# One encoder block on one Trainium2 core: each head's keys written once from PSUM, and copied by DMA to the other half of the partitions

## The chip, the core and the metric

The kernel runs on one core of one Trainium2 chip. A core has TensorE (PE in the profile; weight loads have a row of their own, PEld), VectorE (DVE), ScalarE (ACT), GpSimd (POOL), and SyncE (SP), which here issues nearly all DMA transfers. PE writes to PSUM, ACT and DVE read it there, and both write to SBUF, the working memory of 128 partitions. The engines run side by side, each through its own instructions in a fixed order, and wait for each other by semaphores. The metric is device time in microseconds (us) for one execution of the whole block.

## The reference

One layer of a bidirectional encoder on 1024 positions of width 1024, batch 1, in float32. What matters here is the mixing half:

```python
h = rmsnorm(x, g_mix[i]) * (1 + scale1) + shift1
proj = h @ w_in[i]
qa, ka, va, qb, kb, vb, ga, gb = jnp.split(proj, split_at, axis=-1)
oa = mixture_of_dilations(heads(qa, 8), heads(ka, 8), heads(va, 8), rel_bias)
ob = neighbourhood_attention_2d(heads(qb, 8), heads(kb, 8), heads(vb, 8), na_rpb[i])
merged = sigmoid(ga) * (oa @ w_branch_dil[i]) + sigmoid(gb) * (ob @ w_branch_na[i])
x = x + gate1 * (merged @ w_out[i])
```

Eight heads of 64 channels attend in three dilated windows, merged by their denominators, and eight others in a two-dimensional window of 8 rows by 16 columns on a 16 x 64 grid. The scores are `q . k / 8 + bias`. A gated convolutional feed-forward half of width 2816 and a last RMSNorm follow; the change does not touch them.

## The kernel before

Products are kept near float32 accuracy with operands of 32-bit matmul type split in two: a high part `hi`, the value rounded to that type, and a low part `lo`, the rest. A projection is then three matmuls for each of eight blocks of the contraction (lines 77 to 79): `hi*hi`, `hi*lo` and `lo*hi`, 24 matmuls of 128 x 512 into one PSUM bank, named `pj`. Channels stand on the partitions and positions along the free axis, so one bank is a head pair (two heads of 64 channels) by half of the positions.

Scores use a trick of layout. A head has only 64 channels, so its 128-partition query tile `qs` holds the high part of q on one half of the partitions and the low part on the other. The key tile `ks` holds the high part of k, scaled by 1/8, on both halves, and `kl` the low part of k on both halves. Two matmuls then give all four products (lines 507 and 508, 537 and 538 in the dilated heads, 633 in the neighbourhood heads). For head `i` of a pair, the slice `a` is the half of the partitions on which its channels come out of the projection, and `b` the other half.

So the keys must stand twice in SBUF, and before the change all four are written straight from PSUM: `k_half` (line 390) takes one half of the positions and writes, for each of the two heads, `ks` twice on ACT (line 403) and `kl` twice on DVE (line 405). In the dilated heads a write is 64 x 512 in one run; in the neighbourhood heads the same number of elements is written in another order of grid columns and rows, with strides.

`qk_tiles` does this for one head pair: two halves of the queries, two halves of the keys. For the first pair it alternates query and key halves; for the others it does the queries, then the keys. There are eight pairs, 0 to 3 dilated and 4 to 7 neighbourhood. The loop of line 690 attends to pair n, then projects pair n + 1, then computes some gate tiles (`gate_tile`, line 676), two projections each, counted by `counts`: two tiles for each of the first four pairs, one for each of the next two, none for pair 6 and six for pair 7. The gates' results go to HBM as `gs`.

The PSUM pool `psg` has two banks for all these projections: a third one waits until the first has been read out. The pool `psl` has two banks for scores `S`; DVE adds the bias and takes minima (line 491 dilated, 637 neighbourhood), ACT takes the exponential (492, 639), PE transposes the result `P` into `T`, ACT and DVE split that into `th` and `tl` (496 and 497, 657 and 658), and PE multiplies with the values `vv` into `O`. `qkpool` has three buffers for each of `qs`, `ks` and `kl`, while one pair uses two.

Nobody wrote the order of the engines' instructions here by hand. The first stage (line 260) is in written order; from line 347 on a scheduler works out when it expects each instruction to be ready and merges the attention of pair n with the projections of pair n + 1 and the gates, for each engine, SP included. The order it finds is fixed when the program is built. A change of a few instructions can therefore move many others.

Beside the keys' reads of PSUM, SP's queue near the first pair matters: `vb_chunks` (line 446) copies the neighbourhood heads' values in 32 transfers from one HBM scratch tensor into four others, named `vb`, in the order that the later heads read.

Of the kernel before, what the change touches and what calls it, by code (L numbers as in the profile page):

```python
# [11 lines left out]
AF = mybir.ActivationFunctionType  # L12
OP = mybir.AluOpType
# [15 lines left out]
def hybrid_encoder(tc, xT, c, w_ada, small, w_in, w_v, p1_bias, p23_bias, na_bias, ln2_mult, ident, w_br, w_out,  # L29
                   w_up, w_down, out):  # L30
    nc = tc.nc
    act, dve, pool, pe, sp = nc.scalar, nc.vector, nc.gpsimd, nc.tensor, nc.sync
# [5 lines left out]
    def f(ap):  # L38
        return ap.bitcast(FT)
# [29 lines left out]
    def weights(src, lo_eng):  # L69
        return w_split(w_load(src), lo_eng)  # L70

    def product(psum, w, moving, k0=0, n=KT, ks=None):

        whi, wlo = w
        for k in ks or range(n):
            mhi, mlo = moving(k)
            pe.matmul(psum, whi[:, k0 + k], mhi, start=k == 0, stop=False)  # L77
            pe.matmul(psum, whi[:, k0 + k], mlo, start=False, stop=False)  # L78
            pe.matmul(psum, wlo[:, k0 + k], mhi, start=False, stop=k == n - 1)  # L79
# [89 lines left out]
    def x_load(hf):  # L169
        x = []  # L170
        for kp in range(4):
            t = x_tile() if hf == 0 else wpool.tile([128, S], FT, name=("whi", "wlo")[kp % 2])
            sp.dma_start(t.rearrange("p (a b) -> p a b", a=2), xT[hf, kp])
            x += [t[:, 512 * i:512 * i + 512] for i in range(2)]
        return x
# [84 lines left out]
    with tc.manual_schedule(engines={e.engine for e in (sp, act, dve, pool, pe)}):  # L260
        x = [x_load(0)]
# [49 lines left out]
        for n in range(24):  # L311
# [16 lines left out]
            i = n // 2 - 2  # L328
# [4 lines left out]
            if n % 2 and n >= 9:  # L333
                i = (n - 9) // 2
# [12 lines left out]
    def qk_tiles(br, pr, ws=None):  # L347
        qt, kt = ((0, 4), (12, 16))[br]
        qs = [qkpool.tile([128, S], FR, name="qs") for _ in range(2)]
        ks = [qkpool.tile([128, S], FR, name="ks") for _ in range(2)]  # L350
        kl = [qkpool.tile([128, S], FR, name="kl") for _ in range(2)]
        qb = []

        def q_half(hf, w, p=None):
            cols = halves[hf]
            if p is None:
                p = ps_g.tile([128, 512], FT, name="pj")
                if br == 0:
                    product(p, w, lambda k: h[hf, k])
                else:  # L360
                    q_windows(p, w, hf)
            for i in range(2):
                a, b = slice(64 * i, 64 * i + 64), slice(64 - 64 * i, 128 - 64 * i)
                d, pp = qs[i][:, cols], p
                if br:
                    d = qs[i].rearrange("p (v r t) -> p v r t", v=64, r=4)[:, :, 2 * hf:2 * hf + 2]
                    pp = p.rearrange("p (r v t) -> p v r t", r=2, v=64)
                act.activation(d[a], pp[a], AF.Copy)
                dve.tensor_tensor(d[b], pp[a], f(d[a]), OP.subtract)  # L369

        def q_windows(p, w, hf):

            whi, wlo = w
            for k in range(KT):
                mhi, mlo = (t.rearrange("p (r w c t) -> p r c w t", r=2, w=16, c=4) for t in h[hf, k])
                for x, (ww, m) in enumerate(((whi, mhi), (whi, mlo), (wlo, mhi))):
                    for r in range(2):
                        pe.matmul(p[:, 256 * r:256 * r + 256], ww[:, k], m[:, r], start=k + x + r == 0,  # L378
                                  stop=k == KT - 1 and x == 2, skip_group_check=True)

        def q_blocks():
            for i in range(2):
                q = qkpool.tile([128, S], FR, name="qb", bufs=2)
                for r in range(4):
                    pool.tensor_scalar(q.rearrange("p (b r j) -> p r b j", b=8, r=4)[:, r],  # L385
                                       f(qs[i][:, 256 * r:256 * r + 256]).rearrange("p (b j) -> p b j", b=8), 1.0, None,
                                       OP.mult)
                qb.append(q)

        def k_half(hf, w, p=None):  # L390
            cols = halves[hf]
            if p is None:
                p = ps_g.tile([128, 512], FT, name="pj")
                product(p, w, lambda k: h[hf, k])
            for i in range(2):
                a, b = slice(64 * i, 64 * i + 64), slice(64 - 64 * i, 128 - 64 * i)
                kh, ll, pp = ks[i][:, cols], kl[i][:, cols], p
                if br:
                    kh, ll = (t.rearrange("p (w t r) -> p r w t", w=16, t=16)[:, 2 * hf:2 * hf + 2]
                              for t in (ks[i], kl[i]))  # L400
                    pp = p.rearrange("p (r w t) -> p r w t", r=2, w=16)
                for x in (a, b):
                    act.activation(kh[x], pp[a], AF.Copy, scale=0.125)  # L403
                for x in (a, b):
                    dve.scalar_tensor_tensor(ll[x], pp[a], 0.125, f(kh[a]), OP.mult, OP.subtract)  # L405

        if ws:
            for hf in range(2):
                q_half(hf, ws[0])
                k_half(hf, ws[1])  # L410
            q_blocks()
        else:
            w = weights(w_in[qt + pr], pool)
            for hf in range(2):
                q_half(hf, w)
            if br == 0:
                q_blocks()
            w = weights(w_in[kt + pr], pool)
            for hf in range(2):
                k_half(hf, w)  # L420
        return qs, ks, kl, qb

    def va_load(head, vr):
# [22 lines left out]
    def vb_chunks(cc):  # L446
        for cb in range(4):
            t0, n = NA_T0[cb], NA_NC[cb]
            for r in range(4):
                sp.dma_start(vb_s[cb].rearrange("(w t r) n -> r w t n", r=4, t=n)[r, :, :, cc],  # L450
                             vb_c[256 * r:256 * r + 256, cc].rearrange("(w t) n -> w t n", t=16)[:, t0:t0 + n])

    qk = qk_tiles(0, 0, qk_w)
    ps_l = tc.alloc_tile_pool(name="psl", bufs=2, space=PSUM, reuse_waits="tile")
    ps_a = tc.alloc_tile_pool(name="psa", bufs=2, space=PSUM, reuse_waits="tile")
# [230 lines left out]
    with tc.tile_pool(name="at", bufs=2, reuse_waits="tile") as work:  # L686
        lnm = sm_pool.tile([128, 384], FT, name="lnm", bufs=1)
        sp.dma_start(lnm, ln2_mult)
        counts = (2, 2, 2, 2, 1, 1, 0, 6)
        for n in range(8):  # L690
            (attend_dil, attend_na)[n // 4](n % 4, qk, work)
            if n == 0:
                for hv in range(2):
                    vb_chunks(slice(hv * 256, hv * 256 + 256))
            if n < 7:
                qk = qk_tiles((n + 1) // 4, (n + 1) % 4)
                for t in range(sum(counts[:n]), sum(counts[:n + 1])):
                    gate_tile(t)
# [628 lines left out]
```

## Time and profile before

| | |
|---|---|
| runs: median (lowest to highest) of 3 | 1591.77 us (1590.76 to 1592.05) |
| profiled execution, from first to last instruction | 1588.7 us |
| PE busy | 1513.5 us, 95% |
| DVE, ACT, POOL busy | 1058.9, 804.8, 741.8 us |
| mean granted TensorE clock | 0.980 |
| mean DMA rate | 124 GB/s |

The profile gives of its execution the span from the first to the last instruction and no other time; the runs are timed apart and contain what lies around the span. The mixing half with the keys runs from about 150 to 700 us of the span. A group of instructions is named by line, engine, operation and tiles, with its count, its busy time and the mean of one; the idle time of an engine is listed with what ended it. The granted clock is the share of TensorE's full clock that the chip allowed in a stretch.

### The profile page before, as it was taken

How to read it: one execution, taken by the hardware profiler on the slowest of the kernel's cores; microseconds unless marked ns; L12 is line 12 of the kernel's file. 1: busy time of each engine (PE TensorE's matmuls, PEld its weight loads, DVE VectorE, ACT ScalarE, POOL GpSimd, SP SyncE). 2: the span in 40 equal slices, each digit the busy share in tenths (PEclk: the TensorE clock that was granted, in tenths of full speed). 3: DMA queues.
4: the chain of work that ended last, by engine and by line, in shares of the span. 5: the costliest groups of instructions: out<-in, count | busy, mean ns of one | idle time of the engine just before them, and what ended most of it. 6: DMA issues, size and time to landing. Idle time of an engine off the chain costs nothing.

```text
span 1588.7 us, 21184 instructions
## 1 busy us (share of the span) xinstructions
PE 1513.5 (95%) x7582; PEld 1273.0 (80%) x7582; DVE 1058.9 (67%) x1905; ACT 804.8 (51%) x1451; POOL 741.8 (47%) x475
## 2 busy tenths in 40 slices
PE   8998999999998999999899889999999999999998
PEld 7787888888887988888678777788888887778787
DVE  7694457676667666535532898876666667787765
ACT  3420666675756766634334445444444446475542
POOL 2310423432214433411236768676666665588621
PEclk8999999999999999999999999999999999999999
DMA  9477522322223443546544312222222223433313
GB/s 376 185 287 264 140 72 72 101 68 79 67 76 112 140 107 105 173 129 209 159 144 154 113 53 80 80 95 92 80 80 80 80 82 137 153 128 131 113 54 106
DMA packets 107442, 196.81 MB, mean 124 GB/s; under 512 B 39845, under 2 KB 55077, under 8 KB 107301
## 3 DMA queue, kind: packets, MB, share of 16 engines
q1 hardware_dynamic: 107064, 195.20, 37.3%
q8 instruction: 59, 0.97, 0.3%
q14 instruction: 47, 0.38, 0.1%
q10 hardware_dynamic: 272, 0.26, 0.1%
HBM read 158.73 MB, written 42.47 MB: 127 GB/s over the span
## 4 chain that ended last, share of the span: by engine, by line
PE 63%; DVE 14%; DMA 6%; ACT 6%; POOL 5%; issue 5%; SPq 1%; DVEq 0%; ACTq 0%; POOLq 0%
PE pj L817 9%; PE pj L816 9%; PE pj L818 9%; PE pj L77 8%; PE pj L79 8%; PE pj L78 8%; DVE mt L151 2%; DMA g<-gs 2%; DVE big L1012 2%; PE pj L378 2%; ACT ks L403 2%; DMA wraw<-w_down 2%; PE O L666 1%; POOL wlo L56 1%; DVE kl L405 1%
## 5 line engine op out<-in xcount | busy, mean ns | idle before, releaser
L56 POOL TENSOR_TENSOR wlo<-wraw,whi 128x1024 fp32r<-128x1024 f32 (+1 forms) x77 | 179.8, 2336 | 289.9 <-ACT whi L55 277.9
L77 PE MATMUL pj<-h,whi 128*128 128x512 f32 x448 | 179.9, 402 | 8.9 <-DVE kl L405 7.0
L78 PE MATMUL pj<-h,whi 128*128 128x512 f32 x448 | 178.4, 398 | 0.0
L79 PE MATMUL pj<-h,wlo 128*128 128x512 f32 x448 | 178.1, 398 | 0.0
L56 POOL TENSOR_TENSOR wsl<-big,wsh 128x1024 fp32r<-128x1024 f32 (+1 forms) x45 | 109.4, 2432 | 50.2 <-ACT wsh L55 50.1
L1012 DVE SCALAR_TENSOR_TENSOR big<-wc,sm,big 128x256 f32<-128x256 f32 (+1 forms) x132 | 117.0, 934 | 17.3 <-ACT big L1006 17.2
L55 ACT ACTIVATE whi<-wraw 128x1024 fp32r<-128x1024 f32 (+1 forms) x79 | 80.7, 1021 | 83.3 <-POOL wc L957 20.3
L77 PEld LDWEIGHTS pj<-h,whi 128*128 128x128 f32 x448 | 85.0, 190 | 25.6 <-issue 5.1
L79 PEld LDWEIGHTS pj<-h,wlo 128*128 128x128 f32 x448 | 84.8, 189 | 15.7
L78 PEld LDWEIGHTS pj<-h,whi 128*128 128x128 f32 x448 | 85.2, 190 | 15.0
L491 DVE CUSTOM_DVE_ANT_0 P<-S,bias 128x256 f32<-128x256 f32 x128 | 52.3, 421 | 55.5 <-PE S L538 40.2
L405 DVE SCALAR_TENSOR_TENSOR kl<-pj,ks 64x512 fp32r<-64x512 f32 x64 | 56.5, 883 | 43.8 <-ACT ks L403 40.0
L443 POOL TENSOR_TENSOR vv<-vv 96x256 fp32r<-96x256 f32 (+2 forms) x32 | 40.9, 1286 | 95.6 <-ACT vv L442 79.4
L492 ACT ACTIVATE P<-P,st 128x256 f32<-128x256 f32 x128 | 64.3, 503 | 39.7 <-DVE st L491 39.2
L1012 DVE SCALAR_TENSOR_TENSOR big<-pj,sm,big 128x512 f32<-128x512 f32 x132 | 67.9, 565 | 16.1 <-ACT big L1006 16.1
L385 POOL TENSOR_SCALAR qb<-qs 128x256 fp32r<-128x256 f32 x32 | 26.4, 851 | 105.9 <-DVE qs L369 51.1
L1006 ACT ACTIVATE big<-wc,sm 128x512 f32<-128x512 f32 x44 | 35.8, 816 | 76.6 <-DVE wc L829 46.0
L644 POOL TENSOR_SCALAR P<-P,stb 128x288 f32<-128x288 f32 (+1 forms) x32 | 40.4, 1263 | 66.1 <-DVE stb L641 60.4
L56 POOL TENSOR_TENSOR wsl<-wraw,wsh 128x768 fp32r<-128x768 f32 (+1 forms) x23 | 49.9, 2169 | 43.3 <-ACT wsh L55 39.1
L403 ACT ACTIVATE ks<-pj 64x512 fp32r<-64x512 f32 x64 | 53.7, 838 | 21.1 <-DVE kl L405 10.0
L1038 ACT ACTIVATE big<-big 128x1024 f32<-128x1024 f32 x22 | 23.3, 1060 | 79.7 <-DVE big L1012 79.7
L55 ACT ACTIVATE wsh<-big 128x1024 fp32r<-128x1024 f32 (+1 forms) x45 | 44.8, 999 | 36.4 <-POOL big L781 21.9
(366 smaller groups left out, 4864.8 us busy)
## 6 DMA issues: line engine op xcount, KB each, us to landing
wraw<-w_in SPq DMA_DIRECT2D x32, 512.0 KB, 3.8
t<-w_ada SPq DMA_DIRECT2D x24, 512.0 KB, 7.8
big<-w_up SPq DMA_DIRECT2D x22, 512.0 KB, 5.2
wraw<-w_up SPq DMA_DIRECT2D x22, 512.0 KB, 3.5
as<-big SPq DMA_DIRECT2D x22, 512.0 KB, 2.6
big<-as SPq DMA_DIRECT2D x22, 512.0 KB, 6.1
wraw<-w_down SPq DMA_DIRECT2D x24, 384.0 KB, 3.8
x<-w_ada SPq DMA_DIRECT2D x16, 512.0 KB, 8.9
```

Source lines behind the costliest of these rows:

```text
L55: act.activation(hi, raw, AF.Copy)
L56: lo_eng.tensor_tensor(lo, raw, f(hi), OP.subtract)
L77: pe.matmul(psum, whi[:, k0 + k], mhi, start=k == 0, stop=False)
L78: pe.matmul(psum, whi[:, k0 + k], mlo, start=False, stop=False)
L79: pe.matmul(psum, wlo[:, k0 + k], mhi, start=False, stop=k == n - 1)
L403: act.activation(kh[x], pp[a], AF.Copy, scale=0.125)
L405: dve.scalar_tensor_tensor(ll[x], pp[a], 0.125, f(kh[a]), OP.mult, OP.subtract)
L492: act.activation(pp, pp, AF.Exp, bias=mi, scale=-1.0, accum_out=li)
L816: pe.matmul(psum, whi[:, k], bhi, start=j < 4 and k == 0, stop=False, skip_group_check=True)
L817: pe.matmul(psum, whi[:, k], blo, start=False, stop=False, skip_group_check=True)
L818: pe.matmul(psum, wlo[:, k], bhi, start=False, stop=k == n - 1, skip_group_check=True)
L1012: dve.scalar_tensor_tensor(y[:, dst], src, wt, y[:, dst], OP.mult, OP.add)
```

## The change

Each head's keys are written once: `ks` by one ACT instruction and `kl` by one DVE instruction per half of the positions, on the half `a` alone. When both halves of the positions are there, the new function `k_copies` has SP issue four DMAs for the pair, 64 partitions by 1024 elements (256 KB) each: `ks` and `kl` of head 0, then of head 1, from the half `a` to the half `b` of the same tile. It is called behind the two halves of the keys, for the first pair ahead of `q_blocks`. Line numbers behind the change are larger by 6; `ks` is written in line 402, `kl` in 403, and the copies are line 409.

```diff
-                for x in (a, b):
-                    act.activation(kh[x], pp[a], AF.Copy, scale=0.125)
-                for x in (a, b):
-                    dve.scalar_tensor_tensor(ll[x], pp[a], 0.125, f(kh[a]), OP.mult, OP.subtract)
+                act.activation(kh[a], pp[a], AF.Copy, scale=0.125)
+                dve.scalar_tensor_tensor(ll[a], pp[a], 0.125, f(kh[a]), OP.mult, OP.subtract)
+
+        def k_copies():
+            for i in range(2):
+                a, b = slice(64 * i, 64 * i + 64), slice(64 - 64 * i, 128 - 64 * i)
+                for t in (ks[i], kl[i]):
+                    sp.dma_start(f(t[b]), f(t[a]))
 
         if ws:
             for hf in range(2):
                 q_half(hf, ws[0])
                 k_half(hf, ws[1])
+            k_copies()
             q_blocks()
...
             for hf in range(2):
                 k_half(hf, w)
+            k_copies()
         return qs, ks, kl, qb
```

The scheduler moves instructions on all engines. Three places are shown. The first is PE at the start of the first pair, before the change: `pj_1198` is the second half of the pair's queries, `pj_1227` the second half of its keys, `ks_1132` and `kl_1134` the keys of head 0.

```order
L79 MATMUL pj_1198<-h_614,wlo_874 128x512
L507 MATMUL S_1301<-ks_1132,qs_1130 128x256
L507 MATMUL S_1325<-ks_1132,qs_1130 128x256
L508 MATMUL S_1301<-kl_1134,qs_1130 128x256
L508 MATMUL S_1325<-kl_1134,qs_1130 128x256
L77 MATMUL pj_1227<-h_573,whi_877 128x512
```

With the change, `pj_1223` is the second half of the keys, and `pj_1842` and `pj_1871` are the two halves of the next pair's queries; rows within a projection are left out.

```order
L79 MATMUL pj_1223<-h_614,wlo_878 128x512
L77 MATMUL pj_1842<-h_244,whi_1838 128x512
...
L77 MATMUL pj_1871<-h_573,whi_1838 128x512
...
L78 MATMUL pj_1871<-h_597,whi_1838 128x512
L513 MATMUL S_1297<-ks_1132,qs_1130 128x256
L513 MATMUL S_1321<-ks_1132,qs_1130 128x256
L79 MATMUL pj_1871<-h_596,wlo_1839 128x512
L514 MATMUL S_1297<-kl_1134,qs_1130 128x256
```

The first scores stood ahead of the second half of the keys; now they stand behind it, behind all of the next pair's first half of queries and 14 matmuls of its second.

The second place is SP about the same time, with the change: `vb` are the neighbourhood value copies, and the weights of a gate tile come last.

```order
L456 DMA vb1_83<-vbc_81 128x1x256 x2
L456 DMA vb2_84<-vbc_81 128x1x256 x2
L456 DMA vb3_85<-vbc_81 96x1x256
L409 DMA ks_1132<-ks_1132 64x1024
L409 DMA kl_1134<-kl_1134 64x1024
L409 DMA ks_1133<-ks_1133 64x1024
L409 DMA kl_1135<-kl_1135 64x1024
L456 DMA vb3_85<-vbc_81 96x1x256
L60 DMA wraw_1978<-w_in 128x1024
```

Before, the thirteen `vb` transfers of this group and the weight load followed each other; now the four key copies stand behind the twelfth.

The third place is ACT in pair 6, at the second half of its keys, before the change:

```order
L55 ACTIVATE whi_6071<-wraw_6069 128x1024
L403 ACTIVATE ks_5467<-pj_5622 64x2x256 x2
L403 ACTIVATE ks_5468<-pj_5622 64x2x256 x2
L657 ACTIVATE th_5373<-T_5368 96x512
L672 ACTIVATE u1_5119<-O_5271 64x16x4x4
```

and with it:

```order
L55 ACTIVATE whi_6043<-wraw_6041 128x1024
L402 ACTIVATE ks_5443<-pj_5594 64x2x256
L402 ACTIVATE ks_5444<-pj_5594 64x2x256
L663 ACTIVATE th_5349<-T_5344 96x512
L678 ACTIVATE u1_5095<-O_5247 64x16x4x4
```

The order is the same and each pair of writes has become one; DVE's row of `kl` stands likewise between the same neighbours as before.

## The prediction

> **What bounds the kernel now.** I read the page's engine sums first, then its chain of waits, then the stage in which the changed lines run.
>
> ```profile
> span 1588.7 us, 21184 instructions
> PE 1513.5 (95%) x7582; PEld 1273.0 (80%) x7582; DVE 1058.9 (67%) x1905; ACT 804.8 (51%) x1451; POOL 741.8 (47%) x475
> PE 63%; DVE 14%; DMA 6%; ACT 6%; POOL 5%; issue 5%; SPq 1%; DVEq 0%; ACTq 0%; POOLq 0%
> ```
>
> TensorE (PE) is busy for 95% of the span and carries 63% of the chain. Its instructions are the same after the change, so the time moves only by what PE waits for. Busy time taken from ScalarE (ACT) or VectorE (DVE) is worth nothing by itself. The question is which PE waits stand behind the key evictions, and which new ones the copies bring.
>
> How much eviction there is, by lines and in two stretches (us of the span, busy time and count, clock, DMA share, GB/s): ACT's line 403, then DVE's line 405. The first stretch holds the four dilated pairs, the second the four neighbourhood pairs.
>
> ```profile
> 157.00:395.00 238.00, 18.92 (x32) 1.00 0.30 89
> 395.00:640.00 245.00, 34.73 (x32) 0.97 0.35 99
> ...
> 157.00:395.00 238.00, 22.04 (x32) 1.00 0.30 89
> 395.00:640.00 245.00, 34.49 (x32) 0.97 0.35 99
> ```
>
> One eviction takes 0.59 (ACT) and 0.69 us (DVE) in a dilated pair, 1.09 and 1.08 us in a neighbourhood pair, where keys are written with strides. Half of them go: 26.8 us of ACT, 28.3 us of DVE.
>
> Who makes PE wait (us in total, times, longest), first 395 to 640 us, then the row of 157 to 395 us:
>
> ```profile
> PE pj L77 <- DVE kl L405: 6.6, 5, 1.7
> PE S L507 <- DVE st L491: 2.4, 1, 2.4
> PE O L666 <- ACT th L657: 1.6, 1, 1.6
> PE O L521 <- ACT th L496: 0.7, 1, 0.7
> ...
> PE pj L77 <- DVE kl L405: 0.4, 1, 0.4
> ```
>
> The first row is the eviction's own: a projection waits for its PSUM bank until DVE has read the keys out of it, 7.0 us with the last row. The three between hide the same cause, as the timeline of two places shows (start, length, engine, line; in brackets the idle time and its releaser), the first about pair 6, the second about pair 4:
>
> ```profile
> 563.12 2.15 ACT L403 ACTIVATE ks<-pj 64x512 fp32r<-64x512 f32 x2
> 565.30 2.19 DVE L405 SCALAR_TENSOR_TENSOR kl<-pj,ks 64x512 fp32r<-64x512 f32 x2 [2.44 <-ACT ks L403]
> 567.52 2.15 ACT L403 ACTIVATE ks<-pj 64x512 fp32r<-64x512 f32 x2 [2.25 <-DVE kl L405]
> 569.69 0.59 ACT L657 ACTIVATE th<-T 96x512 fp32r<-96x512 f32 x1
> 569.70 2.13 DVE L405 SCALAR_TENSOR_TENSOR kl<-pj,ks 64x512 fp32r<-64x512 f32 x2 [2.21 <-ACT ks L403]
> 570.34 0.38 PE L666 MATMUL O<-th,vv 96*128 96x256 f32 x1 [1.60 <-ACT th L657]
> 571.98 0.77 PE L77 MATMUL pj<-h,whi 128*128 128x512 f32 x1 [1.26 <-DVE kl L405]
> ...
> 434.23 2.14 DVE L405 SCALAR_TENSOR_TENSOR kl<-pj,ks 64x512 fp32r<-64x512 f32 x2 [3.68 <-ACT ks L403]
> 437.61 0.41 DVE L491 CUSTOM_DVE_ANT_0 P<-S,bias 128x256 f32<-128x256 f32 x1
> 438.08 0.39 PE L507 MATMUL S<-ks,qs 128*128 128x256 f32 x1 [2.41 <-DVE st L491]
> ```
>
> ACT and DVE take turns on one bank: two writes, two, two, two, 8.7 us from 563.12 to 571.83. Everything behind them in their queues stands still: the copy `th` at 569.69 for which PE idles 1.60 us, the softmax at 437.61 for which it idles 2.41 us. After both places the granted clock is halved (the seventh number; busy times of PE, PEld, DVE, ACT and POOL before it):
>
> ```profile
> 438.50:445.50 7.00, 6.33 (x23) 5.45 (x23) 6.16 (x15) 4.05 (x13) 2.70 (x3) 0.51 0.10 37
> 571.50:575.00 3.50, 3.02 (x7) 2.47 (x8) 3.03 (x9) 2.06 (x6) 0.73 (x1) 0.52 0.00 0
> ```
>
> That loses 0.49 of 7.0 and 0.48 of 3.5 us: 3.4 and 1.7 us of PE.
>
> **What the change takes away.** With one write per head, the turns at 563.12 are one, one, one, one: 4.35 us. ACT's and DVE's orders at this place are otherwise as before, so `th` comes about 4.3 us earlier, and the bank is free at about 567.5. A gate projection is 24 matmuls long, 5.5 us (between the two S rows of the next fence), so a 4.35 us eviction fits behind one where 8.7 us does not. Bank waits: at most 7.0, I take 6.5. Waits behind blocked queues: at most 2.4 + 1.6 + 0.7 = 4.7; I take 3.0, since another operand can be late next. Clock: at most 5.1; I take 2.0, because other idle time of PE can halve it too. **Gain 11.5 us**, between 7.0 (the eviction's own rows alone) and 16.8.
>
> **What it adds.** 32 DMAs of 256 KB, 8.4 MB, on SP, each waiting on DVE or ACT. The first scores of a pair now need both whole copies of head 0. The order says what PE has in between. Pairs 1 to 4: at least four gate projections, 22 us; pairs 5 and 6: two, 11 us; pair 7: one, 5.5 us; pair 0: what is worked out below. The chain from the end of the last key projection is 1.1 + 1.1 us to `kl` of head 0, about 0.4 us for each issue, and a landing, for which the nearest rows are these (KB, us from issue to landing), one to and one from HBM:
>
> ```profile
> gs<-gs SPq DMA_DIRECT2D x21, 256.0 KB, 2.0
> bias<-p_bias SPq DMA_DIRECT2D x8, 256.0 KB, 2.8
> ```
>
> That makes 5 to 6 us: hidden in pairs 1 to 6, about level in pair 7 (I charge 0.5 us, 0 to 2). What stands behind a waiting copy on SP, a weight load and the values' loads, stands late enough in the order; sharing the DMA engines costs the rest, 0.5 us.
>
> **Pair 0** is the exception, because its copies stand on SP behind twelve of the neighbourhood value copies. Rows of the timeline there, and DMA share (last but one) in two stretches; the last row is a stretch further on:
>
> ```profile
> 164.81 0.40 PE L507 MATMUL S<-ks,qs 128*128 128x256 f32 x2
> 170.79 0.28 PE L507 MATMUL S<-ks,qs 128*128 128x256 f32 x1
> 173.70 0.47 PE L77 MATMUL pj<-h,whi 128*128 128x512 f32 x1 [1.10 <-DVE qs L369]
> 169.21 0.59 ACT L368 ACTIVATE qs<-pj 64x512 fp32r<-64x512 f32 x1
> 173.81 1.04 ACT L55 ACTIVATE whi<-wraw 128x1024 fp32r<-128x1024 f32 x1
> 174.88 1.19 ACT L403 ACTIVATE ks<-pj 64x512 fp32r<-64x512 f32 x2
> 171.12 0.51 ACT L492 ACTIVATE P<-P,st 128x256 f32<-128x256 f32 x1
> 170.42 8.27 SPq L450 DMA_DIRECT2D vb<-vbc  x13
> 178.79 13.36 SPq L60 DMA_DIRECT2D wraw<-w_in  x3
> 179.00:182.00 3.00, 3.00 (x19) 2.65 (x19) 2.92 (x8) 2.29 (x6) 3.00 (x2) 1.00 0.84 207
> 182.00:185.00 3.00, 3.00 (x14) 2.44 (x13) 0.88 (x2) 0.47 (x2) 0.00 (x0) 1.00 0.70 218
> 202.80:209.60 6.80, 4.98 (x36) 4.13 (x34) 5.70 (x18) 6.65 (x16) 5.64 (x6) 1.00 0.21 67
> ```
>
> In the new order PE runs the second key projection at 164.8 (where the first scores stood) to 170.3, waits for the bank of the queries until about 171.1 (two turns of 0.59 and 0.69 us from 169.21, with no exponential between them), and ends pair 1's first query projection at 176.6. The next one needs the bank of the keys, evicted from 174.9 in four turns to 177.5, and after 14 of its 24 matmuls (3.2 us) come the first scores: **180.7**. The copies are issued behind twelve of the thirteen rows of 170.42 (0.64 us each), from 178.1 on. The DMA engines are still filled by those (share 0.84), and 512 KB, the first two copies, take about 2 us at 207 to 218 GB/s plus the landing: about 183.7. PE waits **3.0 us** (0 if the copies overtake, 5.0 if all four must be through).
>
> Behind it comes a second cost. The new order has spent its projections before the first scores, so four query blocks follow without one. Until the next projection gets its bank, ACT does one weight split (1.04), five exponentials (0.55 each), two copies of transposed blocks and three query evictions (0.59 each), 6.7 us, and DVE its half of the last eviction (0.69). PE's own work in there is worth some 34 matmuls of 256 columns, at half of a 512-column one (5.5 / 24 / 2 = 0.115 us) 3.9 us. It idles for 7.4 - 3.9 = 3.5 us (2.5 to 5.0); 1.5 us come back because the gap of 202.80 to 209.60, 1.8 us of idling, is filled by a projection in the new order. Net **2.0 us**.
>
> Sum: -11.5 + 3.0 + 2.0 + 0.5 + 0.5 = **-5.5 us**: a span of 1583.2. The runs' median of 1591.77 lies 3.1 us above the span, and I keep that: **1586.3 us**.
>
> [...]
>
> **The rivals.**
>
> *Pair 0 starves (slower).* If the first copies land at 186, PE idles 5.0 us, then 5.0 us in the four blocks with nothing given back, and two such gaps halve the clock as at 438.5 (3.4 us). With 1.0 us for pair 7 and sharing that is 14.4 us; a gain of only 8.0 (bank waits, 1.5 behind queues) leaves +6.4: 1598 us. For it: the vb rows and the filled DMA engines, and idle gaps that did halve the clock. Against it: a single place of 30 us. It decides from about 12 us lost there.
>
> *The waits change hands (no change).* PE finds the bank free but waits for the softmax at the same places, since ACT and DVE must still do the same attention work: gain 6.0, cost 6.0, 1591.8 us. For it is this row of the waits over the whole span, which the change does not touch. Against it: at 563 the two queues hold nothing else in the way.
>
> ```profile
> ACT P L492 <- DVE st L491: 39.2, 35, 2.9
> ```
>
> *All of it (more).* The copies come in time in pair 0 and the clock stays up: -16.8 + 2.0 + 0.5 = -14.3, 1577.5 us. Against it: SP's order.
>
> **How the numbers follow.** Forecast 0.42 (own range 1582 to 1588.6), starving 0.20, changing hands 0.22, all of it 0.16. A difference below 0.2%, 3.2 us, can't be told from none. Faster than 1588.6 is the forecast and the last rival: 0.58; within it 0.22; slower 0.20. The range for eight in ten runs from the last rival to just under the slower one: 1577 to 1597.
>
> **What would show it.** ACT's key eviction at 32 instructions of about 0.84 us, DVE's at 32; the row of PE waiting for `kl` gone or below 1 us; no half clock about 438 and 571; a PE wait on a DMA of `ks` or `kl` of 2 to 4 us near 181 and none above 1 us later. Two or more pairs that wait for copies, or PE's waits on softmax growing by more than 5 us, would make the prediction wrong.

## The result, and the profile after

The changed kernel takes **1574.8 us** (median; 1572.4 to 1577.1) where the kernel before takes 1591.3 us: a ratio of 0.9897, 95% interval 0.9882 to 0.9911. It is faster, as forecast, but by 16.5 us where 5.5 were forecast, and 2.2 us below the range. The page of the changed kernel (span, busy times, shares of the chain of waits):

```profile
span 1570.5 us, 21187 instructions
PE 1505.5 (96%) x7582; PEld 1267.3 (81%) x7582; DVE 1035.6 (66%) x1873; ACT 779.1 (50%) x1419; POOL 740.6 (47%) x475
PE 64%; DVE 12%; DMA 8%; POOL 6%; issue 4%; ACT 4%; SPq 1%; DVEq 0%; ACTq 0%; POOLq 0%
```

The span is 18.2 us shorter, and PE is still the bound. DVE and ACT each lose two points of the chain (26 us of ACT and 23 of DVE are no longer busy), DMA gains two. Who makes PE wait between 384 and 680 us, with the busy times, the clock and the DMA share of the same stretch, in the kernel before:

```profile
PE pj L77 <- DVE kl L405: 6.6, 5, 1.7
PE S L507 <- DVE st L491: 4.3, 2, 2.4
PE S L633 <- DVE stb L637: 1.8, 2, 1.6
PE O L666 <- ACT th L657: 1.6, 1, 1.6
PE T L654 <- DVE tl L658: 0.8, 2, 0.6
PE pj L77 <- DVE qs L369: 0.8, 1, 0.8
PE O L521 <- ACT th L496: 0.7, 1, 0.7
PE S L537 <- DVE st L491: 0.2, 1, 0.2
...
384.00:680.00 296.00, 278.95 (x1738) 248.75 (x1737) 197.40 (x489) 195.77 (x421) 111.57 (x82) 0.98 0.38 112
```

and in the changed kernel:

```profile
PE S L639 <- DVE stb L643: 3.1, 2, 1.7
PE S L513 <- DVE st L497: 1.9, 1, 1.9
...
384.00:680.00 296.00, 291.01 (x1855) 261.25 (x1854) 184.64 (x485) 186.37 (x418) 113.75 (x83) 1.00 0.48 133
```

Six of eight rows are gone, the eviction's own among them. PE waits 5.0 us where it waited 16.8, and in the same 296 us it starts 1855 matmuls instead of 1738.

The turns on the bank in pair 6, rows of the timeline of ACT and DVE with the change, against those of 563.12 to 571.83 before:

```profile
553.75 1.06 ACT L402 ACTIVATE ks<-pj 64x512 fp32r<-64x512 f32 x1
555.96 1.07 ACT L402 ACTIVATE ks<-pj 64x512 fp32r<-64x512 f32 x1 [1.15 <-DVE kl L403]
557.06 0.60 ACT L663 ACTIVATE th<-T 96x512 fp32r<-96x512 f32 x1
...
554.84 1.08 DVE L403 SCALAR_TENSOR_TENSOR kl<-pj,ks 64x512 fp32r<-64x512 f32 x1 [1.78 <-ACT ks L402]
557.07 1.08 DVE L403 SCALAR_TENSOR_TENSOR kl<-pj,ks 64x512 fp32r<-64x512 f32 x1 [1.14 <-ACT ks L402]
...
552.00:560.00 8.00, 8.00 (x48) 6.97 (x47) 4.68 (x9) 5.51 (x9) 3.51 (x2) 1.00 0.70 163
```

One, one, one, one, from 553.75 to 558.15: 4.40 us where it was 8.71. `th` follows 3.31 us after the first write instead of 6.57, and PE has no idle time in the 8 us around (last row).

Where the time went is seen best at equal amounts of PE's work. PE streams the same columns in both kernels, only in another order; the table gives the time between the points at which it has started so many thousand columns of the moving operand, worked out from the start times of all 7582 matmuls of each profiled execution.

| columns started (thousands) | what runs there | before | after | difference |
|---|---|---|---|---|
| 242 to 290 | start of pair 0 | 24.8 | 29.9 | +5.1 |
| 290 to 672 | rest of the dilated pairs 0 to 3 | 194.2 | 193.5 | -0.7 |
| 672 to 816 | projections of pair 4, end of pair 3 | 83.4 | 73.7 | -9.7 |
| 816 to 1224 | neighbourhood attention, projections of pairs 5 to 7 | 217.2 | 205.1 | -12.1 |
| 1224 to 1680 | gates and what follows, not touched | 227.5 | 224.9 | -2.6 |

So the change gains 21.8 us where the neighbourhood keys are written (672 to 1224 thousand, called the neighbourhood stretch below: 300.6 us before, 278.8 after) and gives 5.1 us back in pair 0. One profiled execution stands behind each number, and the runs of one kernel lie 3 to 14 us apart, so differences of a few us in a stretch are not to be read. The -2.6 us is of that kind: in code that no kernel here touches, the fifteen kernels of the next section spread from 221.6 to 227.5 us.

### The profile page after: what moved, and what is told of

It reads as the page before. It is cut to its first block, busy times and chain, and to the rows that moved or that the text cites. A ratio compares the mean times of both kernels' runs of the same rounds, so it can differ in the third digit from the quotient of the medians.

```text
span 1570.5 us, 21187 instructions
## 1 busy us (share of the span) xinstructions
PE 1505.5 (96%) x7582; PEld 1267.3 (81%) x7582; DVE 1035.6 (66%) x1873; ACT 779.1 (50%) x1419; POOL 740.6 (47%) x475
## 4 chain that ended last, share of the span: by engine, by line
PE 64%; DVE 12%; DMA 8%; POOL 6%; issue 4%; ACT 4%; SPq 1%; DVEq 0%; ACTq 0%; POOLq 0%
PE pj L822 8%; PE pj L823 8%; PE pj L824 8%; PE pj L79 8%; PE pj L77 8%; PE pj L78 8%; DMA g<-gs 2%; DMA wraw<-w_down 2%; PE pj L378 2%; DVE mt L151 2%; DVE big L1018 2%; PE O L672 2%; POOL wsl L56 2%; POOL wlo L56 1%; PE T L660 1%
## 5 line engine op out<-in xcount | busy, mean ns | idle before, releaser
L55 ACT ACTIVATE whi<-wraw 128x1024 fp32r<-128x1024 f32 (+1 forms) x79 | 80.7, 1022 | 73.7 <-PE pj L78 30.0
L385 POOL TENSOR_SCALAR qb<-qs 128x256 fp32r<-128x256 f32 x32 | 26.4, 851 | 124.0 <-PE S L544 57.9
L1018 DVE SCALAR_TENSOR_TENSOR big<-pj,sm,big 128x512 f32<-128x512 f32 x132 | 67.9, 565 | 16.1 <-ACT big L1012 16.1
L503 DVE TENSOR_TENSOR tl<-T,th 128x512 fp32r<-128x512 f32 x64 | 43.7, 688 | 23.9 <-ACT th L502 23.5
L840 DVE TENSOR_TENSOR pj<-pj,wc 128x512 f32<-128x512 f32 x34 | 23.7, 696 | 47.0 <-PE pj L824 46.9
```

Source lines behind the costliest of these rows:

```text
L55: act.activation(hi, raw, AF.Copy)
L503: dve.tensor_tensor(tl, pt, f(th), OP.subtract)
L1018: dve.scalar_tensor_tensor(y[:, dst], src, wt, y[:, dst], OP.mult, OP.add)
```

## The experiments

Three theories: **T1**, the length of ACT's and DVE's turns on a projection's bank in the neighbourhood pairs sets the time (8.7 us before, 4.35 with single writes); **T2**, the gain is the other order that the scheduler found; **T3**, it goes in proportion to the engine time saved, wherever it is saved. All edits are to `k_half` and `k_copies`, if nothing else is said. The summary, with the neighbourhood stretch and the start of pair 0 (242 to 290 thousand columns) of each profiled execution:

| kernel | turn, us | pair 0 start | neighbourhood stretch | time, us | ratio to before |
|---|---|---|---|---|---|
| before | 8.7 | 24.8 | 300.6 | 1591.3 | |
| the change | 4.35 | 29.9 | 278.8 | 1574.8 | 0.9897 [0.9882, 0.9911] |
| neighbourhood pairs only | 4.35 | 24.2 | 279.8 | 1569.5 | 0.9874 [0.9851, 0.9897] |
| dilated pairs only | 8.7 | 30.2 | 292.3 | 1586.1 | 0.9984 [0.9963, 1.0005] |
| four writes and the copies | 8.7 | 31.4 | 293.8 | 1590.8 | 1.0001 [0.9983, 1.0019] |
| all pairs but the first | 4.35 | 26.4 | 287.6 | 1574.9 | 0.9909 [0.9883, 0.9935] |
| each write made twice | 8.7 | 24.7 | 295.4 | 1587.5 | 0.9976 [0.9952, 0.9999] |
| pair 0's copies from ACT | 4.35 | 32.2 | 287.6 | 1581.4 | 0.9933 [0.9907, 0.9960] |
| four writes in one run | 5.1 | 24.4 | 281.4 | 1569.8 | 0.9860 [0.9826, 0.9894] |
| one write in one run | 2.6 | 24.6 | 277.5 | 1566.2 | 0.9848 [0.9808, 0.9889] |
| one run, reading with stride | 5.1 | 24.9 | 283.7 | 1574.0 | 0.9909 [0.9885, 0.9933] |
| the same, single writes | 2.6 | 24.4 | 284.2 | 1573.2 | 0.9893 [0.9862, 0.9925] |
| ks twice, kl once | 6.5 | 23.9 | 287.1 | 1572.4 | 0.9876 [0.9856, 0.9896] |
| ks once, kl twice | 6.5 | 24.1 | 285.5 | 1575.8 | 0.9897 [0.9872, 0.9922] |
| the change, weights first | 4.35 | 27.8 | 284.9 | 1573.7 | 0.9897 [0.9873, 0.9922] |

Each kernel was timed beside the kernel before, whose median in those runs lay between 1588.6 and 1592.0 us; the ratio and the gains below go by that, the times of two rows by themselves can be off by some us.

Part of the neighbourhood stretch is the clock. PE stood at half clock for 13.7 us of it before (6.8 us lost) and not at all with the change; in the other rows for 0 to 10.2 us. With that loss taken off, the stretch takes 290.3 to 293.8 us in the four kernels with turns of 8.7 us, 281.8 and 283.9 with 6.5, and 277.5 to 284.2 in those with 5.1 and less. So the step down from 8.7 us stays, while the rows from 6.5 us down differ among themselves by as much as their turns could explain.

### One part alone: neighbourhood pairs, dilated pairs, copies without the saving

The neighbourhood pairs alone (`br` is 1 there):

```diff
-                for x in (a, b):
+                for x in (a, b) if br == 0 else (a,):
```

for both loops, and the copies for these pairs only.

> Single writes and copies in the four neighbourhood pairs alone; the dilated pairs write their keys four times from PSUM as before. Theory 1 (the gain is the shorter turn of ACT and DVE on the bank where the writes are strided, 8.7 us against 4.35): all of the gain and none of the cost of pair 0, 20 us under the kernel before, about 1571. Theory 2 (the gain is the scheduler's other order, which starts with the later first scores): most of it gone, within 5 us of the kernel before. Theory 3 (the gain goes with the engine time taken away, wherever it is): 63% of that time is here, 10 us under.

1569.5 us: the whole gain, without the loss in pair 0 (24.2 us there). Expected by T1.

The dilated pairs alone (`br == 1` in that line):

> Single writes and copies in the four dilated pairs alone; the neighbourhood pairs as before. Theory 1: no gain, and the wait for the first copies and the gap behind it remain: 2 to 6 us slower than before, about 1595. Theory 2: 8 to 16 us faster, since the order at the start of the attention is that of the full change. Theory 3: 37% of the gain, 6 us faster.

1586.1 us, no difference that the interval can tell (T3's 6 us stand at its edge). T1 expected a loss; pair 0 does lose 5.4 us, but the neighbourhood stretch, whose writes are as before, comes out 8.3 us shorter. The clock is 5.1 of that: 3.4 us at half clock against 13.7. The other 3 us are what the order that the scheduler finds can have moved, so little of T2 is left here. And the dilated pairs save half of their evictions, 9.5 us of ACT and 11.0 of DVE, while the rest of these pairs (290 to 672 thousand columns) takes 193.6 us for 194.2: engine time by itself is worth next to nothing, against T3.

Four writes and the copies:

```diff
+                for x in (a, b) if True else (a,):
...
+            k_copies()
```

> All four writes from PSUM are kept and the copies are made too, over the same values: the evictions as long as before, the waits for copies and their DMA traffic as with the change. Theory 1: nothing gained, and the cost of the copies alone shows: 4 to 8 us slower than before, about 1597. Theory 2: near the changed kernel, 8 to 16 us faster. Theory 3: 2 to 6 us slower.

1590.8 us, as before. T2 had expected 8 to 16 us faster and falls as the main cause; T1 had expected 4 to 8 us slower, and that did not come either. In the profiled execution two things cancel: the start of pair 0 takes 6.6 us more than before, and the neighbourhood stretch 6.8 less, of which 5.1 are the clock (3.4 us at half clock against 13.7). Who makes PE wait between 384 and 680 us in this kernel:

```profile
PE pj L77 <- DVE kl L405: 5.7, 5, 1.7
...
PE S L642 <- DMA ks<-ks: 0.9, 1, 0.9
```

The row of the eviction is there again, five times and 1.7 us long at most, as before. A copy makes PE wait there in one place, 0.9 us, and in two more at the start of pair 0 (157 to 384 us):

```profile
PE S L516 <- DMA ks<-ks: 1.7, 1, 1.7
...
PE S L517 <- DMA kl<-kl: 0.7, 1, 0.7
```

### The same order, shorter writes

Only the layout of the neighbourhood keys is changed; four writes, no copies. The kernel leaves out the permutation of the keys to grid columns, so it does not compute the reference:

```diff
-                if br:
-                    kh, ll = (t.rearrange("p (w t r) -> p r w t", w=16, t=16)[:, 2 * hf:2 * hf + 2]
-                              for t in (ks[i], kl[i]))
-                    pp = p.rearrange("p (r w t) -> p r w t", r=2, w=16)
```

> The kernel before with one thing changed: in the neighbourhood pairs the keys are written in the order in which they come out of the projection, in one run, not permuted to grid columns (this leaves the permutation of the keys out of the computation). All four writes stay, there are no copies, and every engine's order of instructions is the same as in the kernel before; only the writes get shorter (1.09 and 1.08 us to about 0.59 and 0.69), and the turn on a bank falls from 8.7 to about 5.1 us. Theory 1 (length of the turns): 10 to 16 us faster than before, 1576 to 1582. Theory 2 (the order): no change, within 3 us.

1569.8 us, 21.8 us faster: the cleanest of the tests, since every engine's order is that of the kernel before. Of the schedule nothing is changed but the length of a write (0.59 and 0.69 us for 1.09 and 1.08), and the gain is the whole of it; T2 expected no change. T1's own figure was too small again. The first neighbourhood scores in the kernel before, then here (duration in ns: least, median, most; first and last start):

```profile
L633 PE MATMUL S<-ks,qs x64: 290/338/447, 467.0 to 666.3; 128*128 128x288 f32 x32, 128*128 128x384 f32 x32
```

```profile
L629 PE MATMUL S<-ks,qs x64: 290/338/443, 459.0 to 646.5; 128*128 128x288 f32 x32, 128*128 128x384 f32 x32
```

The same matmuls begin 8.0 us earlier and end 19.8 us earlier. The row of PE waiting for `kl` is gone, as with the change:

```profile
PE S L503 <- DVE st L487: 1.6, 1, 1.6
PE S L629 <- DVE stb L633: 1.1, 2, 0.9
PE pj L77 <- DVE qs L369: 0.8, 1, 0.8
PE S L533 <- DVE st L487: 0.2, 1, 0.2
```

Both shortenings together, single writes in one run with copies in the neighbourhood pairs:

> The kernel with single writes and copies in the neighbourhood pairs alone, and there too the keys written in one run (permutation of the keys left out of the computation); its order is that of the kernel with single writes in the neighbourhood pairs. The turn falls from 4.35 to about 2.6 us. Theory 1, with the limit where a turn is shorter than one projection of 5.5 us: nothing more to gain, 0 to 4 us below that kernel's 1569.5. If every microsecond of ACT and DVE counts (theory 3): 7 us below it.

1566.2 us, some 3 us below the neighbourhood pairs alone, and the intervals of the two overlap. Another 2 us off a turn that is already shorter than a projection (5.5 us) brings little.

### How the gain depends on the turn

The neighbourhood pairs alone, but each of the single writes made twice over the same half, so that the turn is as long as before and the copies are there:

```diff
+                for x in (a, b) if br == 0 else (a, a):
```

> Copies in the neighbourhood pairs alone, as in the first experiment, but there each write from PSUM is made twice, over the same half: the turns are 8.7 us again while the scores wait for the copies. Theory 1: the gain is gone, 1586 to 1596. Theory 2: it stays, 1568 to 1576.

1587.5 us: 18 of the 22 us are gone again. PE's waits (384 to 680 us):

```profile
PE O L530 <- ACT th L505: 3.7, 2, 3.1
...
PE S L642 <- DMA kl<-kl: 2.1, 1, 2.1
PE pj L77 <- DVE kl L405: 1.7, 3, 0.7
```

The waits behind ACT's and DVE's blocked queues are back. PE also waits 0.7 us for a copy of `ks` and 2.1 us for one of `kl`, which are issued only when the second write has ended, and a half clock of 3.4 us follows at 514.9. So some 4.5 us of this kernel's loss can be the later copies and not the bank; its neighbourhood stretch is 15.6 us longer than that of the neighbourhood pairs alone.

Two turns of 6.5 us, `ks` twice and `kl` once, and the reverse, with copies of the one that is written once:

> Neighbourhood pairs: ACT writes ks twice per head as before, DVE writes kl once, and two DMAs per pair copy kl to the other half; dilated pairs as before. The turns on one bank are then two, one, two, one: 6.5 us, between the 8.7 us of the kernel before and the 4.35 us of single writes (which gave 1569.5 us). If the gain goes in proportion to the turn: half of 22 us, 1578 to 1583. If only what exceeds a projection of 5.5 us counts (3.2 us of excess before, 1.0 us here): two thirds or more of it, 1573 to 1577. If the order that the scheduler finds for fewer writes made the gain: no statement but that it may be anything.

> The reverse: ACT writes ks once and two DMAs per pair copy it, DVE writes kl twice. Turns one, two, one, two: also 6.5 us. In proportion to the turn 1578 to 1583, by the excess over a projection 1573 to 1577. If DVE's share of the turn is what holds others up (its softmax instructions stand behind it, as at 437.6): above the run with ks twice; if ACT's is (the copy th at 569.7): below it.

1572.4 and 1575.8 us, 19.6 and 16.1 us faster than before. Half of the shortening brings 0.73 and 0.89 of the 22.1 us of single writes. That is not proportion; the rule by the excess over a projection of 5.5 us (3.2 us before, 1.0 here: 15 us) is nearer and still a little low for `ks` twice. PE's waits for `th` and for the bank (384 to 680 us), `ks` twice first, `kl` twice second:

```profile
PE O L675 <- ACT th L666: 3.2, 2, 1.8
...
PE pj L77 <- DVE kl L405: 0.2, 1, 0.2
```

```profile
PE pj L77 <- DVE kl L405: 5.4, 3, 3.0
```

Whichever engine has two writes shows in its own row: with `ks` twice the copies `th` on ACT come late, with `kl` twice the bank. Which of the two is worse isn't told apart by the intervals.

### A kernel without copies

The scores can take the keys from a tile in natural order, if the matmul reads them with stride:

```diff
-            kv, lv = (t.rearrange("p (w c) -> p w c", w=16) for t in (ks[i], kl[i]))
+            kv, lv = (t.rearrange("p (r w t) -> p w t r", r=4, w=16) for t in (ks[i], kl[i]))
...
-                        pe.matmul(d, qs[i][:, qc], t[:, 4 * R:4 * R + 12, 4 * t0:4 * t0 + 4 * n], start=x_ == 0,
+                        pe.matmul(d, qs[i][:, qc], t[:, 4 * R:4 * R + 12, t0:t0 + n], start=x_ == 0,
```

> The kernel before with the neighbourhood keys written in one run (positions in their natural order), four writes per half as before, and no copies; the reordering that the writes did is now in the reading: the scores' matmuls take their 288 or 384 key columns from the tile with a stride of 256 elements, in the same order of columns as before. Computes all of the reference; the order of instructions is that of the kernel before on all engines. If only the length of ACT's and DVE's turns on the bank counts: as with the contiguous writes alone, 1566 to 1574. If TensorE pays for the strided columns: up to twice the 0.34 us of each of the 128 matmuls of line 633, 43 us more, 1610 to 1615; in between if it pays for a part.

> The same reading with stride, neighbourhood keys written once in one run and copied to the other half by four DMAs per pair; dilated pairs as before. Computes all of the reference. Turn length on the bank 2.4 us against 4.8 us with the four contiguous writes. If both turns fit behind a projection of 5.5 us, little is left to gain: 1563 to 1570, 0 to 6 us below the run with four contiguous writes and the same reading. If every microsecond of a turn counts: 9 to 12 us below it.

1574.0 and 1573.2 us. The first is as fast as the change, with an edit of layout alone and no DMA. It pays a part for the reading; the scores here:

```profile
L629 PE MATMUL S<-ks,qs x64: 324/390/492, 457.2 to 648.2; 128*128 128x288 f32 x32, 128*128 128x384 f32 x32
```

0.390 us against 0.338, and 0.369 against 0.337 for `kl`: over 64 matmuls each some 5 us. That is of the size by which it is slower than the run without the stride (4.2 us between the medians, 7 us between the gains over the kernel before). Single writes on top bring 0.7 us, within the expectation of 0 to 6. The fastest kernel that computes all of the reference is thus the neighbourhood pairs alone, 1569.5 us; its interval and that of the change overlap, and the 5.3 us between them are of the size of what pair 0 loses.

### Pair 0

The start of pair 0 in the changed kernel, rows of the timeline of SP, ACT and PE, and a stretch at the end:

```profile
168.78 8.38 SPq L456 DMA_DIRECT2D vb<-vbc  x12
177.27 0.53 SPq L409 DMA_DIRECT2D ks<-ks  x1
...
181.57 9.88 SPq L60 DMA_DIRECT2D wraw<-w_in  x3
...
182.08 0.39 PE L513 MATMUL S<-ks,qs 128*128 128x256 f32 x2
...
187.59 1.06 ACT L55 ACTIVATE whi<-wraw 128x1024 fp32r<-128x1024 f32 x1 [3.05 <-DMA wraw<-w_in]
189.67 1.39 PE L520 MATMUL T<-idt,P 128*128 128x128 f32 x6 [2.38 <-ACT P L498]
...
188.50:192.00 3.50, 2.33 (x12) 2.15 (x13) 1.94 (x8) 3.50 (x13) 2.37 (x1) 0.74 0.00 0
```

The keys are there in time, but only just: the first scores start at 182.08 without a wait, and the copies of `ks` and `kl` of head 0 landed at 181.26 and 182.17. PE itself came late, since it had waited 1.36 us at 173.71 for split weights (`wlo` on POOL). What comes late behind the scores is the next weight load, which SP issues at 181.57 behind the four copies. ACT waits 3.05 us to split it, the exponentials stand behind that on ACT, PE idles 2.38 us for them, and the clock falls (0.74).

All pairs but the first:

```diff
+                for x in (a, b) if ws else (a,):
```

> As the change, but the first pair writes its keys four times from PSUM and makes no copies. Theory 1: the cost of pair 0 (4 to 7 us in the trace) is gone and the gain stays: 1568 to 1571, faster than the changed kernel. Theory 2: the first scores move back, and with them most of the gain goes: 1583 to 1591. Theory 3: a seventh of the dilated pairs' share is lost and the cost of pair 0 too: about 1571.

1574.9 us, where 1568 to 1571 was expected. The start of pair 0 recovers 3.5 us, and would be about back at the 24.8 us of the kernel before but for a half clock of 3.4 us in it. But the order changes, and in the neighbourhood stretch stand 10.2 us at half clock that the change doesn't have, 5.1 of the 8.8 us by which it is longer (this profiled execution, 1578.5 us, is the slowest of its four). One of them:

```profile
483.00:486.50 3.50, 3.50 (x10) 2.69 (x9) 3.40 (x6) 1.91 (x6) 3.13 (x2) 0.50 0.95 320
```

Pair 0's copies issued by ACT, so that SP's queue holds none of them:

```diff
-                    sp.dma_start(f(t[b]), f(t[a]))
+                    (act if ws else sp).dma_start(f(t[b]), f(t[a]))
```

> The full change, with the first pair's four copies issued by ACT and not by SP, so that they need not stand behind the neighbourhood value copies. If SP's queue made the first scores late: 1 to 4 us below the changed kernel, 1571 to 1574. If the gap behind the first scores (no projection left to fill it) is what costs: no change, within 2 us of 1574.8, since the scores come earlier and the gap with them.

1581.4 us, slower than the change. ACT is held by its own issues: before the first copy, and with it before the second `ks`, it waits 2.35 us, until a `vb` transfer has landed. So the copies still waited for the value copies, and the test says nothing on SP's queue:

```profile
176.51 0.52 ACTq L409 DMA_DIRECT2D ks<-ks  x1
177.08 0.59 ACT L402 ACTIVATE ks<-pj 64x512 fp32r<-64x512 f32 x1 [2.35 <-DMA vb<-vbc]
```

The last test moves the weight load alone. With the value copies called one pair later (`if n == 1:` in the loop of line 698 of the changed kernel), the scheduler puts one weight load ahead of the four copies and one value copy behind them; the other engines' orders are those of the change but for one pair of score matmuls.

> The change, with the neighbourhood value copies called for one pair later. The scheduler's order of PE (but for one pair of score matmuls), ACT, DVE and POOL is that of the change; on SP one weight load now stands ahead of the four key copies of pair 0, where it stood behind them, and one value copy behind them. If pair 0 loses its 5 us because this load came late (ACT waits 3.05 us for it with the exponentials behind it, and PE 2.38 us for these, and the half clock behind that): ACT's wait for the load is gone, PE's wait before the transposes at 189.7 falls below 1 us, no half clock near 190, and the time is 3 to 5 us below that of the change, 1569.5 to 1572. If it loses them because four query blocks follow without a projection, or because the keys come later: the wait of PE stays at 2 us or more, 1573 to 1577. If the load now delays the copies: a PE wait on a DMA of ks near 182, 1575 to 1580.

Rows of its timeline of SP and ACT, and the two longest rows of who makes PE wait from 157 to 384 us:

```profile
173.69 0.53 SPq L60 DMA_DIRECT2D wraw<-w_in  x1
...
183.61 1.06 ACT L55 ACTIVATE whi<-wraw 128x1024 fp32r<-128x1024 f32 x1
...
PE pj L77 <- DVE qs L369: 1.5, 1, 1.5
PE pj L79 <- POOL wlo L56: 1.3, 1, 1.3
```

ACT no longer waits for the load (no bracket), PE's wait of 2.38 us and the half clock near 190 are gone: the link from the load to PE's wait is shown. But the gain of 3 to 5 us did not come. The start of pair 0 takes 27.8 us, 2.1 less than with the change (1.7 of it the half clock) and 3.0 more than before, and the time, 1573.7 us where 1569.5 to 1572 was expected, can't be told from the change's. So the load explains about 2 of pair 0's 5 us; the other 3 stay open with the two waits of the last rows near them: for the split weights on POOL (1.4 us with the change) and for the queries' bank. The neighbourhood stretch takes 284.9 us where the change's took 278.8, at the same order and the same writes: 3.4 us of that are half clocks (about 396 and 484), and PE's waits from 384 to 680 us are 7.5 us instead of 5.0.

## Why the prediction was right in sign and wrong in size

**The bound, the place and the mechanism** held: PE bounds, the time moves by PE's waits, and the turns of ACT and DVE on a neighbourhood key bank are what makes it wait. ACT's key evictions are 32, with a median of 0.82 us, and DVE's are 32. The row of PE waiting for `kl` is gone, and so are the half clocks about 438 and 571. The tests with the same order and with the turn lengthened again show it.

**The step that failed is the size of the gain: 11.5 us, "between 7.0 and 16.8"; the neighbourhood stretch gained 21.8.** Term by term, the rows of 384 to 680 us:

- Bank waits, 6.5 forecast: 6.6 in the row before, none after. Right.
- Waits behind the blocked queues, 3.0 forecast: the other seven rows sum to 10.2 us before and 5.0 after, so 5.2. The discount for "another operand can be late next" was too large.
- Clock, 2.0 forecast of at most 5.1: this is the largest miss. The kernel before has a third stretch at half clock, from about 394 on (3.4 us, so 1.7 lost; its rows stand in the last section), beside the two named (3.4 and 1.7): 6.8 us, and none is left in this stretch of the change. The discount "other idle time of PE can halve it too" was not wrong as a mechanism: the kernels with half clocks at 396 and 484 show it, and the change's profiled execution, 1572.4 us, is the fastest of its four. That it cost nothing here is in part luck: the third stretch follows a wait that the change keeps (1.94 and 1.93 us), and the last section shows how the place of the wait differs between the two.
- Short gaps, not in the sum at all: the 3.2 us that are left of the 21.8. The idle rows leave out part of each gap, since the matmuls' ends are modelled; gaps of 0.1 to 0.6 us between the matmuls' streaming, by their starts, add up to some 9 us before and 5 after, which is of this size.

0.1 + 2.2 + 4.8 + 3.2 is the 10.3 us by which the term was too small. The ceiling was too low for two reasons that the rows could have told: the stretch was cut at 395, which left out the half clock that begins at 394, and only rows were counted whose tie to the eviction was seen. 21.8 itself is the difference of two profiled executions; the medians of the runs lie 16.5 us apart.

**Pair 0 was right in size (5.0 forecast, 5.1 measured) by luck, and wrong in kind.** The keys were forecast to be late by 3.0 us (wanted at 180.7, there at about 183.7); they cost nothing, since the copy of `kl` landed at 182.17 and PE, held up by a wait of 1.36 us for split weights that no term of the sum had, reached the scores at 182.08. The sentence that failed is that a weight load behind the copies "stands late enough in the order": it was that load which ACT waited for. The wait among the four query blocks without a projection was forecast in the right place, but it began with the load. The 1.5 us that were to come back later are 0.7 in the table (the rest of the dilated pairs).

**Pair 7 and the sharing of the DMA engines**, 0.5 us each: no instruction of the changed kernel is listed as waiting for a copy. The copies took 2.9 to 6.3 us from issue to landing, median 4.1, longer than the two rows taken for them (2.0 and 2.8), and PE's work still hid them. What the sharing costs was not measured by itself.

**The clock in pair 0** has no term in the sum: the waits there were charged nothing for it, and no run shows that a wait there is free. A half clock of 3.4 us (190.21 to 193.62, 1.7 us lost) followed the wait of 2.38 us with the change. The rows of before, with half clocks after idle times of 2.41 and of 1.60 + 1.26 us, had pointed to such a cost.

**The rivals.** "All of it" (1577.5) was nearest: the keys did come in time and the clock did stay up in the neighbourhood stretch, but pair 0 did cost its 5 us, and the gain was larger than its ceiling. "The waits change hands" is refuted: PE's waits other than for `kl` fell from 10.2 to 5.0 us instead of growing by 6. "Pair 0 starves" found its second gap and its half clock, but not its 14 us.

In the sum of the profiled executions: +5.1 in pair 0, -21.8 in the neighbourhood stretch, -0.7 and -2.6 in the two others and +1.8 ahead of and behind the table make the 18.2 us of the span.

## What to carry to other kernels

When two engines take turns on a PSUM bank, set the length of the whole chain of turns against the matmul work that separates two uses of the bank: here the 3.2 us above a projection's 5.5 us, in each of eight turns, went with some 22 us of PE's time (the bank, the queues behind the two engines, the clock), 1.0 us above it with 2.5 to 6, and below it little more was to be had. A stride in the writing that lengthens a write by half or more (here 1.09 us for 0.59 on ACT, 1.08 for 0.69 on DVE) can be the whole problem, and a change of layout may do as much as a new path of copies. Whether a third bank for the projections would do the same was not tried. When DMAs are put into a queue, look for the first transfer behind them that someone waits for, not only for their own readers.

## What the runs showed of the hardware that was not expected

**A write with a stride of four fp32 elements took 1.85 times as long on ACT, and 1.57 times on DVE, which also reads `ks` with that stride**: 64 x 512 elements, in two runs of 256 with that stride, in 1.09 us on ACT and 1.08 on DVE, against 0.59 and 0.69 in one run. The matmul that reads its moving operand with a stride of 256 elements paid far less, 0.390 us for 0.338.

**Idle times of the same length were followed by half clock or not, by where they fell.** The same scores wait 1.94 us at 393.79 in the kernel before and 1.93 us at 399.39 in the changed one. In each of the fifteen traces the clock changes only at times that lie whole multiples of 3.4133 us apart, to within 3 ns. The two windows about the wait, cut at these times, before:

```profile
390.77:394.18 3.41, 1.47 (x13) 1.33 (x13) 3.17 (x18) 1.99 (x4) 0.00 (x0) 1.00 0.40 145
394.18:397.59 3.41, 3.41 (x18) 3.41 (x18) 3.16 (x9) 1.98 (x7) 0.00 (x0) 0.50 0.00 0
```

and with the change:

```profile
395.01:398.42 3.41, 2.46 (x22) 2.26 (x20) 3.18 (x16) 2.26 (x4) 1.01 (x2) 1.00 0.52 154
398.42:401.84 3.42, 2.45 (x21) 2.45 (x22) 3.08 (x10) 2.24 (x5) 0.00 (x0) 1.00 0.01 5
```

Before, the whole wait lies in one window, in which PE is busy for 1.47 of 3.41 us, and the next window runs at half clock. With the change, the edge at 398.42 cuts the wait in two, PE is busy for 2.46 and 2.45 us, and the clock stays up. Over all fifteen traces, from 150 to 700 us: of the windows at full clock in which PE idled for half or more, 22 of 23 were followed by half clock, and of the 2364 others 5. As an estimate from the stretches at half clock before (3.4 and 6.8 us long, so 1.7 and 3.4 us lost): a wait of about 2 us costs itself alone, or 1.7 to 3.4 us more, by where the windows fall. One execution of each kernel was traced, so how often each case comes in one kernel is not shown.

**A DMA issue that waited held its engine**: put on ACT's queue, the first copy, which waited for a `vb` transfer to land, kept ACT idle for 2.35 us.
